# RWKV and HGRN output products: the two heads in turn, one kind of product after the other

## The chip, the cores and the metric

The kernel runs on one NeuronCore of a Trainium2 chip. The metric is the device time of one execution in microseconds (us). TensorE (PE), VectorE (DVE), ScalarE (ACT), GpSimd (POOL) and the DMA queues run side by side, each taking its own instructions in order.

## What is computed

One inference step of a two-layer streaming encoder on 512 prompt tokens and 8 sample streams of 16 tokens, with 1024 columns, all in float32. Layer 0 mixes with RWKV-7 beside forgetting attention, layer 1 with chunk attention beside HGRN2; a gated convolutional FFN follows each. The change touches the products in which RWKV and HGRN2 form their outputs from a part inside a chunk of 64 tokens and a part from the carried state:

```python
# rwkv7: one step of the scan (per head)
s = s * w_t[:, :, None, :] + sa[..., None] * b_t[:, :, None, :] + v_t[..., None] * k_t[:, :, None, :]
y_t = jnp.einsum('bhvk,bhk->bhv', s, r_t)          # sa = s @ a_t, from the state before the step
...
# hgrn2: one chunk of gla_chunkwise
o = jnp.einsum('bhts,bshv->bthv', att, vc) + jnp.einsum('bthk,bhkv->bthv', qc * jnp.exp(b), s)
```

The kernel does both scans chunk by chunk: an output chunk is (values inside the chunk times a masked score matrix) plus (carried state times scaled queries), two products added into one place in PSUM.

## The kernel before

Dense layers run through `linear` (line 359, tile `lin`), which splits each float32 operand into a high and a low float32r part and does three matmuls per block; these fill most of PE's time. Weights come through SP's queue into `wraw` (4 buffers), ACT casts them to `whi` (line 348) and DVE makes `wlo` (line 349), two buffers each.

The recurrences are cut into eight items each: four pairs of heads `p` times two halves of the tokens `hf`. A tile holds a pair of heads, head `h` in partitions `64*h` to `64*h+63`. A half has five units of 64 tokens: five prompt chunks for `hf` 0; three prompt chunks (`npu` = 3) and two units with four sample streams each for `hf` 1. A matmul here has 64 rows or columns in use, so it is given a place in the array, `tile_position=(row, column)`:

- `Y` (lines 800, 802): per chunk and head a product of all 128 rows with `SAV` at (0, 64h), form `128*64` in the profile, and one with the state `Sa` at (64h, 64h), form `64*64`. The first chunk of `hf` 0 has no state, so an `hf` 0 item has 10 + 8 products and an `hf` 1 item 6 + 6.
- `SAs` (line 817): for the sample units, a masked copy of `W1` times each of four states, four products added up, 16 in an item, all `64*64`.
- `Ys` (lines 835, 837): per unit and head one `128*64` product with `SAV` and four `64*64` ones with the states `S0`, 16 columns each: 4 + 16 in an item.
- `O` (lines 1315, 1317) and `Os` (lines 1336, 1338) are HGRN's counterparts, with `64*64` in both kinds.

A float32 product is two MATMUL instructions in the trace. An RWKV item also needs a triangular solve that leaves PE: scores `sc` on PE, a round trip through DRAM, 30 small steps on POOL (lines 681, 683), another trip, `TT` and `D` on DVE (line 755), and with these PE goes on at `P<-D,E` (line 739). The normalisation behind `Ys` goes through `mean` (line 842), behind `Os` through `ms` (line 228); the result is written to DRAM (`ydr`, `zdr`) through SP's queue and read again as `yb`, cast to `yh` by ACT (line 509) for the output projection.

A scheduler with a time model sets each engine's order when the program is built; on the chip that order is fixed.

Of the kernel before, what the change touches and what calls it, by code (L numbers as in the profile page):

```python
# [139 lines left out]
H = (slice(0, 64), slice(64, 128))  # L140
# [374 lines left out]
def mixer0(tc, A, k):  # L515
    nc = tc.nc
    V, S, G, T, dma, mm, fm, P, C = k.V, k.S, k.G, k.T, k.dma, k.mm, k.fm, k.P, k.C
# [9 lines left out]
    with tc.tile_pool(name="mx", bufs=1) as mp:  # L527
# [46 lines left out]
        def us(u):  # L574
            return slice(64 * u, 64 * u + 64)
# [11 lines left out]
        def rwkv(p, hf, r, kz, v, lrt, grt, item):  # L587
# [5 lines left out]
            def wt(name, w=HF, dt=F32):  # L593
                return mp.tile([128, w], dt, tag="w" + stage[0], name=name, bufs={"A": 11, "B": 8, "C": 5}[stage[0]])
# [5 lines left out]
            npu = 5 if hf == 0 else 3  # L600
# [3 lines left out]
            def m1(lhsT, rhs, name):  # L604
                ps = mm(name, stage[0])
                T.matmul(ps[:, 0:HF], lhsT, rhs, start=True, stop=True)
                return ps[:, 0:HF]
# [8 lines left out]
            ps = m1(blk1, rn, "kkn")  # L616
# [23 lines left out]
            AR, BK = AB[:, 0], AB[:, 1]  # L640
# [8 lines left out]
            M = ABM[:, 2:4].rearrange("p a u s t -> p (a u s t)").rearrange("p (u h s t) -> p u h s t", u=5, h=2, s=2)  # L649
            E = mp.tile([128, 5, 2, 64], F32, tag="E", name="E")  # L650
            Cc = mp.tile([128, 5, 16], F32, tag="Cc", name="Cc", bufs=2)
            for (u0, n, prompt) in (((0, 4, 1), (4, 1, 1)) if hf == 0 else ((0, 3, 1), (3, 2, 0))):
                for h in range(2):
                    ps = mm("sc", stage[0])
                    pv = ps.rearrange("p (u s t) -> p u s t", u=4, s=2)
                    for u in range(u0, u0 + n):
                        T.matmul(pv[H[h], u - u0], Bt[H[h], us(u)], AR[H[h], u], start=True, stop=True, tile_position=(64 * h, 64 * h))
                        T.matmul(pv[H[1 - h], u - u0], Kt[H[h], us(u)], AR[H[h], u], start=True, stop=True,
                                 tile_position=(64 * h, 64 * (1 - h)))
# [51 lines left out]
            SAV = mp.tile([128, 5, 2, 64], F32, tag="SAV", name="SAV", bufs=2)  # L711
            ps = mm("trA", stage[0])
# [4 lines left out]
            ps = mm("trV", stage[0])  # L717
            for u in range(5):
                for h in range(2):
                    T.matmul(ps[H[1 - h], us(u)], v[H[h], us(u)], ident[H[h], H[h]], start=True, stop=True,  # L720
                             tile_position=(64 * h, 64 * (1 - h)))
# [3 lines left out]
            for (u0, n) in ((0, 4), (4, 1)):  # L725
                ps = mm("trB", stage[0])
                pv = ps.rearrange("p (u h t) -> p u h t", u=4, h=2)
                for u in range(u0, u0 + n):
                    for h in range(2):
                        T.matmul(pv[H[h], u - u0, h, :], Bh[:, us(u)], ident[:, H[h]], start=True, stop=True, tile_position=(0, 64 * h))  # L730
                        T.matmul(pv[H[1 - h], u - u0, h, :], Kh[:, us(u)], ident[:, H[h]], start=True, stop=True,
                                 tile_position=(0, 64 * (1 - h)))
# [12 lines left out]
            ps = mm("U", stage[0])  # L745
            for u in range(5):
                for h in range(2):
                    T.matmul(ps[H[h], us(u)], M[H[1 - h], u, h, 0, :], SAV[H[1 - h], u, h, :], start=True, stop=True,
                             tile_position=(64 * (1 - h), 64 * h))
# [25 lines left out]
            Sa = [None] * 5  # L775
# [5 lines left out]
            for c in range(npu):  # L781
# [6 lines left out]
                ps = mm("Sn", stage[0])  # L788
# [8 lines left out]
            ps = mm("Y", stage[0])  # L797
            for c in range(npu):
                for h in range(2):
                    T.matmul(ps[H[h], us(c)], SAV[:, c, h, :], M[:, c, h, 1, :], start=True, stop=Sa[c] is None, tile_position=(0, 64 * h))  # L800
                    if Sa[c] is not None:
                        T.matmul(ps[H[h], us(c)], Sa[c][H[h]], AR[H[h], c, 1, :], start=False, stop=True, tile_position=(64 * h, 64 * h))  # L802
            S.copy(y[:, :npt], ps[:, :npt])
            if hf:

                S0 = mp.tile([128, NB, 64], F32, tag="S0", name="S0")
                with tc.issue_after(k.wada):
                    dma(S0, A["st_rw"][p])
                ps = mm("SAs", stage[0])
                for u in (3, 4):  # L810
                    b0 = 4 * (u - 3)
                    W1m = wt("W1m", 256)
                    V.tensor_tensor(W1m.rearrange("p (b t) -> p b t", b=4), W1[:, us(u)].unsqueeze(1).to_broadcast([128, 4, 64]),
                                    C["colb"].rearrange("p (b t) -> p b t", b=4), op=ALU.mult)
                    for h in range(2):
                        for b in range(4):
                            T.matmul(ps[H[h], us(u - 3)], W1m[H[h], 64 * b:64 * b + 64], S0[H[h], b0 + b, :], start=b == 0, stop=b == 3,
                                     tile_position=(64 * h, 64 * h))
                for h in range(2):
                    V.tensor_tensor(SAV[H[h], 3:5, h, :], ps[H[h], 0:128].rearrange("p (u t) -> p u t", u=2),  # L820
                                    W2[H[h], 192:320].rearrange("p (u t) -> p u t", u=2), op=ALU.add)
                ps = mm("Ss", stage[0])
                for u in (3, 4):
                    for h in range(2):
                        Sm = wt("Sm", 256)
                        V.tensor_tensor(Sm.rearrange("p (b v) -> p b v", b=4), SAV[:, u, h].unsqueeze(1).to_broadcast([128, 4, 64]),
                                        C["em16"].unsqueeze(2).to_broadcast([128, 4, 64]), op=ALU.mult)
                        T.matmul(ps[H[h], 256 * (u - 3):256 * (u - 2)], BK[:, u, h, :], Sm, start=True, stop=True, tile_position=(0, 64 * h))
                o = rwo[:, 1:9, :]
                G.tensor_tensor(o, S0, eL[:, 5:13].unsqueeze(2).to_broadcast([128, NB, 64]), op=ALU.mult)  # L830
                V.tensor_tensor(o, o, ps.rearrange("p (b v) -> p b v", b=NB), op=ALU.add)
                ps = mm("Ys", stage[0])
                for u in (3, 4):
                    for h in range(2):
                        T.matmul(ps[H[h], us(u - 3)], SAV[:, u, h, :], M[:, u, h, 1, :], start=True, stop=False, tile_position=(0, 64 * h))
                        for b in range(4):
                            T.matmul(ps[H[h], 64 * (u - 3) + 16 * b:64 * (u - 3) + 16 * b + 16], S0[H[h], 4 * (u - 3) + b, :],
                                     AR[H[h], u, 1, 16 * b:16 * b + 16], start=False, stop=b == 3, tile_position=(64 * h, 64 * h))
                S.copy(y[:, 192:320], ps[:, 0:128])
                dma(A["o_rw"][:, p], rwo)  # L840

# [326 lines left out]
def mixer1(tc, A, k):  # L1168
    nc = tc.nc
    V, S, G, T, dma, mm, fm, P, C = k.V, k.S, k.G, k.T, k.dma, k.mm, k.fm, k.P, k.C  # L1170
# [7 lines left out]
    def us(u):  # L1178
        return slice(64 * u, 64 * u + 64)

    k.lane.next()
    with tc.tile_pool(name="hx", bufs=1) as mp:
# [36 lines left out]
        def hgrn(p, hf, zq, zf, v, zg):  # L1219
            npu = 5 if hf == 0 else 3  # L1220
            stage = ["A"]

            def wt(name, w=HF, dt=F32):
                return mp.tile([128, w], dt, tag="w" + stage[0], name=name, bufs={"A": 16, "B": 9, "C": 7}[stage[0]])
# [19 lines left out]
            b = wt("b")  # L1244
# [33 lines left out]
            for li, m in enumerate((64, 32, 16, 8, 4, 2, 1)):  # L1278
# [15 lines left out]
                ps = each(0, n, sl(lk), sl(lq), "lev")  # L1294
# [6 lines left out]
            ps = each(0, npu, sl(kt), sl(vt), "KV", "B")  # L1301
            Sa = [None] * 5
# [9 lines left out]
            ps = mm("O", stage[0])  # L1312
            for c in range(npu):
                for h in range(2):
                    T.matmul(ps[H[h], us(c)], vt[H[h], us(c)], att[H[h], us(c)], start=True, stop=Sa[c] is None, tile_position=(64 * h, 64 * h))
                    if Sa[c] is not None:
                        T.matmul(ps[H[h], us(c)], Sa[c][H[h]], qt[H[h], us(c)], start=False, stop=True, tile_position=(64 * h, 64 * h))
            S.copy(y[:, :npt], ps[:, :npt])
            if hf:

                S0 = mp.tile([128, NB, 64], F32, tag="S0", name="S0", bufs=1)
                dma(S0, A["st_hg"][p])
                ps = mm("KVs", "B")
                for u in (3, 4):
                    vm = wt("vm", 256)
                    V.tensor_tensor(vm.rearrange("p (b v) -> p b v", b=4), vt[:, us(u)].unsqueeze(1).to_broadcast([128, 4, 64]),
                                    C["em16"].unsqueeze(2).to_broadcast([128, 4, 64]), op=ALU.mult)
                    for h in range(2):
                        T.matmul(ps[H[h], 256 * (u - 3):256 * (u - 2)], kt[H[h], us(u)], vm[H[h]], start=True, stop=True, tile_position=(64 * h, 64 * h))
                o = hgo[:, 1:9, :]  # L1330
                G.tensor_tensor(o, S0, eL[:, 5:13].unsqueeze(2).to_broadcast([128, NB, 64]), op=ALU.mult)
                V.tensor_tensor(o, o, ps.rearrange("p (b v) -> p b v", b=NB), op=ALU.add)
                ps = mm("Os", stage[0])
                for u in (3, 4):
                    for h in range(2):
                        T.matmul(ps[H[h], us(u - 3)], vt[H[h], us(u)], att[H[h], us(u)], start=True, stop=False, tile_position=(64 * h, 64 * h))
                        for j in range(4):
                            T.matmul(ps[H[h], 64 * (u - 3) + 16 * j:64 * (u - 3) + 16 * j + 16], S0[H[h], 4 * (u - 3) + j, :],
                                     qt[H[h], 64 * u + 16 * j:64 * u + 16 * j + 16], start=False, stop=j == 3, tile_position=(64 * h, 64 * h))
                S.copy(y[:, 192:320], ps[:, 0:128])  # L1340
                dma(A["o_hg"][:, p], hgo)
# [195 lines left out]
```

## Time and profile before

| | us |
|---|---|
| median of 3 runs | 2078.92 (2075.33 to 2080.8) |
| the profiled execution | 2068.11 |
| its span, first to last instruction | 2066.3 |
| PE busy | 1973.0 |
| DVE busy | 1213.5 |
| ACT busy | 944.1 |
| RWKV items (first `sc` to last `Ys`) | 98 to 594 |
| HGRN items | 1160 to 1535 |

Busy time of PE counts from an instruction's start to its modelled end, and successive matmuls overlap in it; what a group of matmuls costs is read as the distance from its first start to the next group's first start. Times of the profiled execution lie 10.8 us under the median of the runs.

### The profile page before, as it was taken

The numbers are of one execution on the slowest core, as the hardware profiler recorded it, in microseconds if no ns is written. First come the engines' busy times: TensorE is split into PE (matmuls) and PEld (weight loads), VectorE is DVE, ScalarE is ACT, GpSimd is POOL, SyncE is SP. The second block draws the span as 40 slices with busy tenths as digits, with TensorE's granted clock in tenths as the row PEclk, the third lists the DMA queues.
The fourth block names the chain that finished last, engine by engine and source line by source line (L and its number), as shares of the span: only waits on it lengthen the run. The fifth ranks groups of instructions, "written<-read, shape, count | busy, mean of one in ns | idle before, by whom it ended". The sixth has DMA issues, their size and how long they took to land.

```text
span 2066.3 us, 42482 instructions
## 1 busy us (share of the span) xinstructions
PE 1973.0 (95%) x16860; PEld 1775.5 (86%) x16860; DVE 1213.5 (59%) x2461; ACT 944.1 (46%) x1877; POOL 511.5 (25%) x1090
## 2 busy tenths in 40 slices
PE   6999999999899999999999999998999999999997
PEld 2877777766698799999999888877888999999997
DVE  3755565667667554454457625776768754454455
ACT  3633343444427442342445525555637652352444
POOL 0424352533212111121112200443223321121112
PEclk7999999989999999999999999999999999999998
DMA  8464435458534642222226786456634322222223
GB/s 311 136 221 130 156 98 151 120 122 227 154 108 161 208 141 73 72 77 77 72 83 211 240 257 195 122 147 176 215 96 133 123 72 76 78 67 77 82 80 123
DMA packets 144661, 282.51 MB, mean 137 GB/s; under 512 B 39768, under 2 KB 80064, under 8 KB 144464
## 3 DMA queue, kind: packets, MB, share of 16 engines
q1 hardware_dynamic: 136784, 267.22, 40.7%
q0 software_dynamic: 7680, 12.59, 2.8%
q8 instruction: 133, 2.18, 0.4%
q14 instruction: 64, 0.52, 0.1%
HBM read 247.69 MB, written 32.07 MB: 135 GB/s over the span
## 4 chain that ended last, share of the span: by engine, by line
PE 71%; issue 8%; DMA 8%; DVE 6%; POOL 3%; ACT 3%; SPq 0%; POOLq 0%; DVEq 0%; ACTq 0%
PE lin L359 57%; DMA wada<-in_ada_w_dram 2%; PE ada L251 1%; DVE wlo L349 1%; PE lev L1265 1%; DMA wraw<-in_w_cd_dram 1%; ACT whi L348 1%; PE Y L800 1%; POOL Tt L683 1%; PE Y L802 1%; PE av L1055 1%; DVE nt L317 1%; POOL Ttmp L681 1%; PE ptr L1048 1%; PE qk L1038 1%
## 5 line engine op out<-in xcount | busy, mean ns | idle before, releaser
L359 PE MATMUL lin<-hi,whi 128*128 128x320 f32 x2272 | 718.3, 316 | 12.6 <-ACT whi L348 7.4
L359 PE MATMUL lin<-hi,wlo 128*128 128x320 f32 x2272 | 714.1, 314 | 5.4 <-DVE wlo L349 5.3
L359 PE MATMUL lin<-lo,whi 128*128 128x320 f32 x2272 | 711.8, 314 | 0.0
L349 DVE TENSOR_TENSOR wlo<-wraw,whi 128x1024 fp32r<-128x1024 f32 (+1 forms) x272 | 335.9, 1236 | 345.3 <-ACT whi L348 342.9
L348 ACT CAST whi<-wraw 128x1024 fp32r<-128x1024 f32 (+1 forms) x272 | 279.3, 1027 | 495.0 <-PE lin L359 370.3
L359 PEld LDWEIGHTS lin<-hi,whi 128*128 128x128 f32 x2272 | 432.0, 190 | 37.6 <-ACT whi L348 10.4
L359 PEld LDWEIGHTS lin<-hi,wlo 128*128 128x128 f32 x2272 | 431.4, 190 | 20.2 <-DVE wlo L349 8.7
L359 PEld LDWEIGHTS lin<-lo,whi 128*128 128x128 f32 x2272 | 431.9, 190 | 6.4 <-issue 3.8
L359 PE MATMUL lin<-gh,whi 128*128 128x320 f32 x704 | 218.8, 311 | 2.9 <-ACT whi L348 1.7
L359 PE MATMUL lin<-gl,whi 128*128 128x320 f32 x704 | 218.1, 310 | 0.6 <-DVE gl L451 0.6
L359 PE MATMUL lin<-gh,wlo 128*128 128x320 f32 x704 | 217.9, 310 | 0.6 <-DVE wlo L349 0.5
L433 POOL COPY cvo<-u 128x2 f32<-128x2 f32 x88 | 83.3, 947 | 380.2 <-ACT u L431 380.2
L394 DVE SCALAR_TENSOR_TENSOR x<-lin,ada_cm,x 128x192 f32<-128x192 f32 (+1 forms) x160 | 76.8, 482 | 149.7 <-PE lin L359 148.9
L359 PEld LDWEIGHTS lin<-gh,whi 128*128 128x128 f32 x704 | 132.6, 189 | 4.6 <-ACT whi L348 2.8
L359 PEld LDWEIGHTS lin<-gl,whi 128*128 128x128 f32 x704 | 132.7, 189 | 1.3 <-DVE gl L451 1.1
L359 PEld LDWEIGHTS lin<-gh,wlo 128*128 128x128 f32 x704 | 132.6, 188 | 1.3 <-DVE wlo L349 1.1
L399 POOL TENSOR_TENSOR x<-x,rs 128x128 f32<-128x128 f32 x80 | 49.1, 615 | 306.9 <-DVE rs L397 306.9
L437 DVE SCALAR_TENSOR_TENSOR t<-u,pp,t 128x656 f32<-128x656 f32 x88 | 79.3, 901 | 25.8 <-ACT t L436 25.1
L251 PE MATMUL ada<-wada,csT 128*32 128x256 f32 x768 | 72.3, 422 | 19.2 <-DMA wada<-in_ada_w_dram 19.1
L359 PE MATMUL lin<-yh,whi 128*128 128x320 f32 x256 | 82.6, 325 | 3.9 <-DVE rs L397 1.4
L436 ACT ACTIVATE t<-u,pp 128x656 f32<-128x656 f32 x88 | 82.5, 938 | 7.2 <-ACT u L432 0.4
L1288 POOL TENSOR_TENSOR d<-d,q 128x160 f32<-128x160 f32 (+1 forms) x48 | 36.5, 760 | 190.6 <-ACT d L1287 186.0
(388 smaller groups left out, 3159.2 us busy)
## 6 DMA issues: line engine op xcount, KB each, us to landing
wraw<-in_w_up_dram SPq DMA_DIRECT2D x100, 512.0 KB
wada<-in_ada_w_dram SPq DMA_DIRECT2D x96, 512.0 KB
wraw<-in_w_cd_dram SPq DMA_DIRECT2D x44, 512.0 KB
wraw<-in_w_dn_dram SPq DMA_DIRECT2D x48, 448.0 KB
wraw<-in_w_ab_dram SPq DMA_DIRECT2D x40, 512.0 KB
wraw<-in_w_dn_dram SPq DMA_DIRECT2D x16, 512.0 KB
wraw<-in_w_abo_dram SPq DMA_DIRECT2D x12, 512.0 KB
wraw<-in_w_cdo_dram SPq DMA_DIRECT2D x12, 512.0 KB
```

The costliest lines, as they stand in the source:

```text
L251: T.matmul(ps[32 * j:32 * j + 32, 0:256], csT[:, kk, :], w[:, j * 256:(j + 1) * 256], start=kk == 0, stop=kk == KD - 1, tile_position=(0, ...
L317: V.tensor_tensor(t, xk(h, kk), r, op=ALU.mult)
L348: S.copy(wh[:, :w], r[:, :w])
L349: V.tensor_tensor(wl[:, :w], r[:, :w], wh[:, :w].bitcast(F32), op=ALU.subtract)
L359: T.matmul(ps[:, 0:HF], w[:, (j * nk + kk) * 128:(j * nk + kk + 1) * 128], a(h, kk), start=c == 0, stop=c == 3 * nk - 1)
L394: V.scalar_tensor_tensor(xx[:, :npr], ps[:, :npr], m[:, 16 + o, 0:1], xx[:, :npr], op0=ALU.mult, op1=ALU.add)
L399: G.tensor_tensor(xx[:, npr:], xx[:, npr:], t.rearrange("p b t -> p (b t)"), op=ALU.add)
L433: G.tensor_copy(cvo[:, o, 0, :], u[:, NP:NP + 2])
L436: S.activation(t, u[:, 2:], AF.Identity, scale=pp[:, ow + 88 + o:ow + 89 + o], bias=pp[:, ob + o:ob + o + 1])
L437: V.scalar_tensor_tensor(t, u[:, 1:UW - 1], pp[:, ow + 44 + o:ow + 45 + o], t, op0=ALU.mult, op1=ALU.add)
L681: G.tensor_tensor(tv, Tt[:, 0:n, j:j + 1].to_broadcast([40, n, w]), At[:, j:j + 1, j + 1:16].to_broadcast([40, n, w]), op=ALU.mult)
L1288: G.tensor_tensor(dv[:, :, h2:], dv[:, :, h2:], xq[:, :, h2:], op=ALU.mult)
```

## The change

Inside `Y`, first all `SAV` products of all chunks, both heads in turn, then all products with the state. The first of a head's `SAV` products alone carries `start` (it opens the whole PSUM bank of that head's partitions), the last state product `stop`. `SAs` loops over streams outside and heads inside. `Ys` does its four `SAV` products first, then the 16 with `S0`, heads innermost. `O` does both heads' first product of a chunk, then both heads' second; `Os` a unit's two first products, then its eight others with heads innermost. No product is added or taken away.

```diff
--- before.py
+++ after.py
@@ -797,9 +797,11 @@
             ps = mm("Y", stage[0])
             for c in range(npu):
                 for h in range(2):
-                    T.matmul(ps[H[h], us(c)], SAV[:, c, h, :], M[:, c, h, 1, :], start=True, stop=Sa[c] is None, tile_position=(0, 64 * h))
+                    T.matmul(ps[H[h], us(c)], SAV[:, c, h, :], M[:, c, h, 1, :], start=c == 0, stop=False, tile_position=(0, 64 * h))
+            for c in range(npu):
+                for h in range(2):
                     if Sa[c] is not None:
-                        T.matmul(ps[H[h], us(c)], Sa[c][H[h]], AR[H[h], c, 1, :], start=False, stop=True, tile_position=(64 * h, 64 * h))
+                        T.matmul(ps[H[h], us(c)], Sa[c][H[h]], AR[H[h], c, 1, :], start=False, stop=c == npu - 1, tile_position=(64 * h, 64 * h))
             S.copy(y[:, :npt], ps[:, :npt])
             if hf:
 
@@ -812,8 +814,8 @@
                     W1m = wt("W1m", 256)
                     V.tensor_tensor(W1m.rearrange("p (b t) -> p b t", b=4), W1[:, us(u)].unsqueeze(1).to_broadcast([128, 4, 64]),
                                     C["colb"].rearrange("p (b t) -> p b t", b=4), op=ALU.mult)
-                    for h in range(2):
-                        for b in range(4):
+                    for b in range(4):
+                        for h in range(2):
                             T.matmul(ps[H[h], us(u - 3)], W1m[H[h], 64 * b:64 * b + 64], S0[H[h], b0 + b, :], start=b == 0, stop=b == 3,
                                      tile_position=(64 * h, 64 * h))
                 for h in range(2):
@@ -832,10 +834,12 @@
                 ps = mm("Ys", stage[0])
                 for u in (3, 4):
                     for h in range(2):
-                        T.matmul(ps[H[h], us(u - 3)], SAV[:, u, h, :], M[:, u, h, 1, :], start=True, stop=False, tile_position=(0, 64 * h))
-                        for b in range(4):
+                        T.matmul(ps[H[h], us(u - 3)], SAV[:, u, h, :], M[:, u, h, 1, :], start=u == 3, stop=False, tile_position=(0, 64 * h))
+                for u in (3, 4):
+                    for b in range(4):
+                        for h in range(2):
                             T.matmul(ps[H[h], 64 * (u - 3) + 16 * b:64 * (u - 3) + 16 * b + 16], S0[H[h], 4 * (u - 3) + b, :],
-                                     AR[H[h], u, 1, 16 * b:16 * b + 16], start=False, stop=b == 3, tile_position=(64 * h, 64 * h))
+                                     AR[H[h], u, 1, 16 * b:16 * b + 16], start=False, stop=u == 4 and b == 3, tile_position=(64 * h, 64 * h))
                 S.copy(y[:, 192:320], ps[:, 0:128])
                 dma(A["o_rw"][:, p], rwo)
 
@@ -1313,6 +1317,7 @@
             for c in range(npu):
                 for h in range(2):
                     T.matmul(ps[H[h], us(c)], vt[H[h], us(c)], att[H[h], us(c)], start=True, stop=Sa[c] is None, tile_position=(64 * h, 64 * h))
+                for h in range(2):
                     if Sa[c] is not None:
                         T.matmul(ps[H[h], us(c)], Sa[c][H[h]], qt[H[h], us(c)], start=False, stop=True, tile_position=(64 * h, 64 * h))
             S.copy(y[:, :npt], ps[:, :npt])
@@ -1334,7 +1339,8 @@
                 for u in (3, 4):
                     for h in range(2):
                         T.matmul(ps[H[h], us(u - 3)], vt[H[h], us(u)], att[H[h], us(u)], start=True, stop=False, tile_position=(64 * h, 64 * h))
-                        for j in range(4):
+                    for j in range(4):
+                        for h in range(2):
                             T.matmul(ps[H[h], 64 * (u - 3) + 16 * j:64 * (u - 3) + 16 * j + 16], S0[H[h], 4 * (u - 3) + j, :],
                                      qt[H[h], 64 * u + 16 * j:64 * u + 16 * j + 16], start=False, stop=j == 3, tile_position=(64 * h, 64 * h))
                 S.copy(y[:, 192:320], ps[:, 0:128])
```

The order in which the built program holds PE's instructions, at the first `Y`. Before:

```order
L359 MATMUL lin<-hi_313,wlo 128x320
L800 MATMUL Y<-ABM,SAV 64x64 x3
L802 MATMUL Y<-ABM,St 64x64
L800 MATMUL Y<-ABM,SAV 64x64
L802 MATMUL Y<-ABM,St 64x64
```

Now:

```order
L359 MATMUL lin<-hi_313,wlo 128x320
L800 MATMUL Y<-ABM,SAV 64x64 x10
L804 MATMUL Y<-ABM,St 64x64 x8
L739 MATMUL TT<-T32T,P_1447 64x64 x10
L359 MATMUL lin<-hi_313,whi 128x320
```

The ten `128*64` products stand together (the row's `64x64` is the shape of its moving operand), then the eight with the state; before, the two kinds take turns from the third product on. The next item's `TT` follows both.

PE at the first `Ys` (the number in `S` is the state tile of this item). Before:

```order
L1038 MATMUL qk<-ra 128x256
L1106 MATMUL vts<-c_ident,r_6596 128x128
L835 MATMUL Ys<-ABM,SAV 64x64
L837 MATMUL Ys<-ABM,S_3883 64x16 x4
L835 MATMUL Ys<-ABM,SAV 64x64
L837 MATMUL Ys<-ABM,S_3883 64x16 x4
```

Now:

```order
L1042 MATMUL qk<-ra 128x256
L1110 MATMUL vts<-c_ident,r_6596 128x128
L837 MATMUL Ys<-ABM,SAV 64x64 x4
L841 MATMUL Ys<-ABM,S_3883 64x16 x16
L739 MATMUL W_4363<-U,TT 64x64 x10
```

Four groups of one and four, of which the first two are shown, have become one of four and one of sixteen.

The scheduler's order has also moved elsewhere. In the RWKV stretch no `lin` matmul changes its place against the items, apart from one that changes places with a `mean`, but steps of the sample attention do. In HGRN's second half the attention steps stand up to 48 `lin` matmuls earlier and the last items later: the last `Os` has 6,300 of the program's 9,696 `lin` matmuls ahead of it, where it had 6,250. ACT behind it, where the last `yh` is cast for the second output projection. Before:

```order
L348 CAST whi<-wraw 128x1024
L1216 ACTIVATE sg<-sg 128x320
L348 CAST whi<-wraw 128x1024
L509 CAST yh<-yb 128x320
L348 CAST whi<-wraw 128x1024
L295 ACTIVATE sq<-x_17870 128x320 x3
```

Now:

```order
L348 CAST whi<-wraw 128x1024
L1220 ACTIVATE sg<-sg 128x320
L348 CAST whi<-wraw 128x1024
L295 ACTIVATE sq<-x_17870 128x320 x3
L348 CAST whi<-wraw 128x1024
L295 ACTIVATE sq<-x_17870 128x320
L509 CAST yh<-yb 128x320
L348 CAST whi<-wraw 128x1024
```

The cast of `yh` has one `whi` more ahead of it, and so the first `whi` behind it belongs to a later step of the projection, 24 `lin` matmuls later. On SP some loads of `kc`, `vc` and weights have changed places with the writes of `zdr` there.

## Rows read from the trace of the kernel before

**Rows 1.** The page, part 1: engine, busy us, share of the span, instructions.

```profile
PE 1973.0 (95%) x16860; PEld 1775.5 (86%) x16860; DVE 1213.5 (59%) x2461; ACT 944.1 (46%) x1877; POOL 511.5 (25%) x1090
```

**Rows 2.** Timeline of PE, first `Y`: start, us, line, what, count of instructions.

```profile
200.79 0.45 PE L800 MATMUL Y<-ABM,SAV 128*64 128x64 f32 x6
201.16 0.32 PE L802 MATMUL Y<-ABM,St 64*64 64x64 f32 x2
201.42 0.33 PE L800 MATMUL Y<-ABM,SAV 128*64 128x64 f32 x2
...
204.86 0.22 PE L802 MATMUL Y<-ABM,St 64*64 64x64 f32 x1
204.87 0.80 PE L739 MATMUL TT<-T32T,P 64*64 64x64 f32 x19
205.59 0.41 PE L359 MATMUL lin<-hi,whi 128*128 128x320 f32 x1
```

**Rows 3.** The same view: `Y`, `SAs` and `Ys` of one second-half item.

```profile
464.29 0.33 PE L800 MATMUL Y<-ABM,SAV 128*64 128x64 f32 x2
...
467.37 0.55 PE L1048 MATMUL ptr<-c_ident,ra 128*128 128x128 f32 x3
...
469.30 1.54 PE L817 MATMUL SAs<-S,W1m 64*64 64x64 f32 x32
470.77 0.32 PE L1055 MATMUL av<-ra 128*64 128x128 f32 x1
...
479.51 0.28 PE L835 MATMUL Ys<-ABM,SAV 128*64 128x64 f32 x2
479.72 0.64 PE L837 MATMUL Ys<-ABM,S 64*64 64x16 f32 x8
...
482.75 0.66 PE L1078 MATMUL vt<-c_ident,ra 128*128 128x128 f32 x4
```

**Rows 4.** The same view: begin and end of an `O` and of an `Os`.

```profile
1179.68 0.50 PE L1315 MATMUL O<-att,vt 64*64 64x64 f32 x8
...
1180.92 0.41 PE L359 MATMUL lin<-hi,wlo 128*128 128x320 f32 x1
...
1533.56 0.41 PE L1338 MATMUL Os<-qt,S 64*64 64x16 f32 x5
...
1535.21 0.41 PE L359 MATMUL lin<-yl,whi 128*128 128x320 f32 x1
```

**Rows 5.** The same view: first and last rows of 26 `trB` instructions.

```profile
164.86 0.27 PE L731 MATMUL trB<-c_ident,Kh 128*64 128x64 f32 x1
...
165.55 0.30 PE L730 MATMUL trB<-c_ident,Bh 128*64 128x64 f32 x3
```

**Rows 6.** Stretches, PE alone: from:to us, PE busy (x), granted clock, DMA, GB/s.

```profile
318.00:321.40 3.40, 3.40 (x31) 0.50 0.00 0
...
372.70:376.10 3.40, 3.40 (x16) 0.51 0.00 0
...
434.20:437.40 3.20, 3.20 (x32) 0.50 0.32 102
...
594.60:597.90 3.30, 3.30 (x14) 0.50 0.33 99
```

**Rows 7.** Timeline of PE, POOL and DVE around two `P`: [idle before <- releaser].

```profile
494.65 0.56 PE L739 MATMUL P<-D,E 64*64 64x64 f32 x12 [0.37 <-DVE D L755]
...
484.24 0.69 POOL L706 TENSOR_TENSOR Bh<-Bt,eL 128x192 f32<-128x192 f32 x1 [7.43 <-DVE Bt L646]
...
543.51 0.49 DVE L842 SCALAR_TENSOR_TENSOR y<-mean,y 128x320 f32<-128x320 f32 x1 [3.00 <-PE mean L606]
```

**Rows 8.** Timeline of ACT and PE at the end of the second mixer.

```profile
1551.35 0.46 ACT L509 CAST yh<-yb 128x320 fp32r<-128x320 f32 x1 [2.03 <-DMA yb<-zdr]
...
1552.94 0.38 PE L359 MATMUL lin<-yh,whi 128*128 128x320 f32 x1 [1.05 <-ACT whi L348]
```

**Rows 9.** Waits of SP's queue, 1340 to 1560: us in total, times, longest.

```profile
SPq L1352 <- DVE y L1351: 22.4, 5, 9.2
```

## The prediction

> **What bounds the kernel now.** I read the page's totals first: PE is busy for 95% of the span and no other engine for more than 59% [rows 1]. Time taken from PE therefore counts, unless something stands just behind it. I then read the timeline of PE at the products concerned, not their busy time, since matmuls overlap in it. At the first `Y` the two kinds take turns, and each product's first instruction begins 0.26 us after the last product's (201.16, 201.42) [rows 2]. The next item's `TT`, right behind it on the same engine, is ten products of one form on the two diagonal places in turn: 19 of its instructions end 0.80 after the first begins. With 0.22 for one alone that is 18 steps in 0.58, so 0.032 an instruction and 0.064 a product of two; the last of them begins at 205.45 and the next form at 205.59, so 0.14 lies between runs of different forms [rows 2]. A product in `Y` costs four times a product in `TT`, with the same 64 columns. What differs is that every second one changes the form between `128*64` and `64*64`. Then I looked at the granted clock behind these bursts, and last at what stands close behind PE: the waits at `P`, at the last `yh`, and on SP.
>
> **The change, part by part.** The cost of a run of n products in one form, heads in turn, is taken as 0.064 n, and 0.14 for each change of form.
>
> `Y`, first half: 200.79 to 204.87 is 4.08 us [rows 2]; now 18 x 0.064 + 0.14 = 1.29. That is 2.8 less, 11.2 in four items. `Y`, second half: 464.29 to 467.37 is 3.08 [rows 3]; now 12 x 0.064 + 2 x 0.14 = 1.05, 2.0 less, 8.0 in four.
>
> `Ys`: 479.51 to 482.75 is 3.24 [rows 3]; now 20 x 0.064 + 0.28 = 1.56, 1.7 less, 6.7 in four. Here the 16-column products of one head now stand on one place, eight instructions in 0.64, so about 0.06 each [rows 3]. If taking turns brings nothing at 16 columns, 16 products x 2 x 0.03 x 4 items = 3.8 of the 6.7 is not had. I take the full sum, since `TT` is nearer in all but the columns, and keep the 3.8 for the range.
>
> `SAs`: 469.30 to 470.77 is 1.47 for 16 products, four on one head's place before the other's turn [rows 3]; now 16 x 0.064 + 0.14 = 1.16, so 0.3, 1.2 in four. `Os`: 1533.56 to 1535.21 is 1.65 for 19 of its 20 products [rows 4]; now 1.36, again 1.2 in four. `O`: 1179.68 to 1180.92 is 1.24 for 18 products [rows 4], and the formula gives 1.29: it already runs at that pace with two on one place, and I put it at nothing. Together 11.2 + 8.0 + 6.7 + 1.2 + 1.2 = 28.3 us of PE's time.
>
> The clock: in four stretches that begin at the end of a `Y` or a `Ys`, or within 1.2 us of it, the granted clock is 0.5, the lower level of 1.2 GHz, for about 3.4 us each [rows 6]. Before each PE had spent 3 to 4 us on products that change form. Work done at half the level loses at most half the stretch, 1.7 us, so 6.8 in all. With shorter bursts such falls should become fewer, but other small matmuls stand nearby. Between 0 and 6.8 I take half, 3.4.
>
> What is late next, in the RWKV stretch: POOL's solve and its trips through DRAM run beside PE, and `P` waits for `D`. In the first half no `Y` stands between an item's `sc` and its `P`, so a shorter `Y` moves both alike, and `lin` matmuls follow; I let all 11.2 pass. In the second half two items' `Y`, `SAs` and `Ys` (4.0 each) do stand between another's `sc` and `P`. For the first, `P` already waits 0.37 for `D` [rows 7]; its solve had stopped on POOL, which waited 7.43 for `Bt` of DVE [rows 7], and DVE in its turn takes `SAs` and `Ss` from PE. Part of the chain moves with PE; I take half as lost, 2. For the second, DVE reached `D` only after 3.00 us of waiting for `mean` of PE [rows 7], which comes earlier now; a quarter lost, 1. The bounds are 0 and 8 for the two.
>
> The end of the second mixer: the last `Os` now has 50 more `lin` matmuls ahead of it, and the first `whi` behind the last `yh` on ACT serves a step 24 matmuls later. ACT waited 2.03 for `yb`, and PE 1.05 for the `whi` behind it [rows 8]. From the end of that `Os` at 1535.21 [rows 4] to PE's restart at 1552.94 [rows 8] stand 109 `lin` matmuls, 0.15 us each without the wait. The chain now begins 7.5 later and is needed 3.6 later, so PE waits some 4 more. It could be nothing, if the sample attention ahead of it ends sooner. I take 4. The other moved attention steps and loads, in both mixers, I put at 0 with 5 to either side.
>
> Sum: 28.3 + 3.4 - 3 - 4 = 24.7, call it **25 us**. The profiled execution of 2068.1 becomes 2043; against the median of the runs, 2078.9, the time is **2054 us**. The 10.8 us between the two I carry over unchanged.
>
> **The rivals.** *The two column halves don't run side by side.* The `SAV` products of both heads use all 128 rows, so one head's weights would wait for the other's matmul, and taking turns would bring nothing. The nearest row against it is `trB`, also `128*64` on the two column halves: 26 instructions from 164.86 to 165.85, less 0.22 for the last alone, are 0.031 each [rows 5], the pace of the diagonal places. If it held all the same, the 64 products of `Y` and 16 of `Ys` would stay at 0.26, 80 x 0.196 = 15.7 of the gain would go, and the time would be 2070. The Trainium skill, "TensorE: Matmul & The Clock Gate", section "The mechanism" of its Part 3, says this: a weight load overlaps matmuls in flight only when its row group differs. The rows 5 speak against it here, for row groups of these halves are the same.
>
> *The cover is gone in RWKV's second half.* All of `Y`, `SAs`, `Ys` there, 15.9, turn into waits for DVE and POOL in attention and at `P`. For it: DVE is at 59% over the span [rows 1], and the 0.37 at `P` shows a wait with no slack left [rows 7]. Against it: the 3.00 that DVE waits for PE [rows 7]. Then 11.2 + 1.2 + 3.4 - 4 = 12 is left, and the time is 2067.
>
> *Nothing to be measured.* Each saving turns into a wait for the same chain of DRAM trips, and the end of the second mixer costs its 4: 2073 to 2085. The order shows that the change does what it says on PE, so only waits could undo it, and in the first half `lin` matmuls stand there instead.
>
> *Slower.* On SP in HGRN's second half some weight loads now stand behind writes of `zdr`, which wait for DVE, up to 9.2 us each [rows 9]. If four of them came late by that much and `lin` stood still each time, 37 us would go, 12 more than is won: 2091. It decides once a load is later than the work that the two `whi` buffers hold lasts: 2 x 24 `lin` matmuls, 7 us at 0.15, and attention's matmuls between them. So most of one wait of 9.2 is covered, and that four fall short by all of it is unlikely.
>
> **How the numbers follow.** A measurement of this kernel can tell about 0.3%, 6 us, from no change. My forecast, 2043 to 2063: 0.72. Second half without cover, 2067: 0.12. No overlap of column halves, 2070: 0.04. Nothing to be measured: 0.07. Slower: 0.05. So faster 0.88, same 0.07, slower 0.05. The lower end of the range is all 28.3 + 6.8 with the attention's 5 and no loss, 40: 2039, taken as 2040. The upper end takes in the two cases around 2070: 2070. That leaves out some 1.5 in 10.
>
> **What would show it.** In the changed profile `Y` should go from its first start to the next group's in 1.2 to 1.4 us (first half) and about 1.05 (second), `Ys` in 1.4 to 2.5, `SAs` near 1.16, `O` unchanged. If `Y` keeps over 3 us, the change of form is not what costs, and the sum falls. If they shrink and the time doesn't, PE must show new idle time at `P`, at attention's `ptr` and `av`, or at `lin` behind `whi`. The stretches at 0.5 behind `Y` and `Ys` should be fewer. The wait at the last `yh` should grow to about 5.

## The result and the profile after

The changed kernel takes 2047.38 us (median of 4 runs, 2042.21 to 2056.34); the kernel before, beside it, 2077.12 (4 runs, 2070.67 to 2080.8). The ratio is 0.9864, with a 95% interval of 0.9827 to 0.9902: 1.4% faster, by 20 to 36 us. Forecast were 2054 and a range of 2040 to 2070. The execution that was profiled took 2056.34, the longest of the four, so a difference of two single profiles shows less than the medians do.

Part 1 of the page after, beside [rows 1]:

```profile
span 2054.6 us, 42485 instructions
PE 1938.6 (94%) x16860; PEld 1748.1 (85%) x16860; DVE 1214.3 (59%) x2461; ACT 944.5 (46%) x1877; POOL 522.0 (25%) x1090
```

As many instructions on PE as before, and 34.4 us less busy time. The span is 11.7 shorter in this execution: span less busy time has grown from 93 to 116. So some of it came back as waiting (to 108 in a second profile of the changed kernel), and where it did in RWKV's stretch is shown below.

The timeline of PE after (start, us, line, what, count of instructions), at the first `Y`, which answers to [rows 2]:

```profile
205.38 0.80 PE L800 MATMUL Y<-ABM,SAV 128*64 128x64 f32 x20
206.11 0.68 PE L804 MATMUL Y<-ABM,St 64*64 64x64 f32 x16
206.63 0.46 PE L739 MATMUL TT<-T32T,P 64*64 64x64 f32 x10
```

and at `Y`, `SAs` and `Ys` of second-half items, which answer to [rows 3]:

```profile
456.87 0.57 PE L800 MATMUL Y<-ABM,SAV 128*64 128x64 f32 x12
457.36 0.56 PE L804 MATMUL Y<-ABM,St 64*64 64x64 f32 x12
457.86 0.44 PE L1052 MATMUL ptr<-c_ident,ra 128*128 128x128 f32 x2
...
470.56 0.45 PE L837 MATMUL Ys<-ABM,SAV 128*64 128x64 f32 x8 [0.41 <-DVE rwo L833]
470.94 1.11 PE L841 MATMUL Ys<-ABM,S 64*64 64x16 f32 x32
471.98 0.32 PE L1059 MATMUL av<-ra 128*64 128x128 f32 x1
...
570.89 1.15 PE L819 MATMUL SAs<-S,W1m 64*64 64x64 f32 x32
571.97 0.42 PE L359 MATMUL lin<-yh,wlo 128*128 128x320 f32 x1
```

From the first start to that of the next group `Y` now takes 1.25 us where it took 4.08 (first half), 0.99 where it took 3.08 (second half), `Ys` 1.42 where it took 3.24, `SAs` 1.08 where it took 1.47 (0.98 where another 64*64 group follows; 0.42 less is taken for all). All four first-half `Y` lie at 1.247. An `O` that runs into `lin` takes 1.195 (1.24 before). HGRN's `Os` went from 0.043 us an instruction (1.645 for 38) to 0.033 (0.865 for the last 26), about 0.4 for its 40. The sum of what the bursts lost: 4 x 2.83 + 4 x 2.09 + 4 x 1.82 + 4 x 0.42 + 4 x 0.4 = 11.3 + 8.4 + 7.3 + 1.7 + 1.6 = 30.3 us. Forecast were 28.3.

### The profile page after: what moved, and what is told of

It is laid out like the page before. It is cut to its first block, busy times and chain, and to the rows that moved or that the text cites. A ratio compares the mean times of both kernels' runs of the same rounds, so it can differ in the third digit from the quotient of the medians.

```text
span 2054.6 us, 42485 instructions
## 1 busy us (share of the span) xinstructions
PE 1938.6 (94%) x16860; PEld 1748.1 (85%) x16860; DVE 1214.3 (59%) x2461; ACT 944.5 (46%) x1877; POOL 522.0 (25%) x1090
## 5 line engine op out<-in xcount | busy, mean ns | idle before, releaser
L1292 POOL TENSOR_TENSOR d<-d,q 128x160 f32<-128x160 f32 (+1 forms) x48 | 41.8, 870 | 179.4 <-ACT d L1291 179.4
```

The lines of the kernel that those rows point to most:

```text
L1292: G.tensor_tensor(dv[:, :, h2:], dv[:, :, h2:], xq[:, :, h2:], op=ALU.mult)
```

## Experiments

Nine kernels ran besides. Each was timed beside the kernel before on the same chip. In the table the gain is what the ratio lacks of 1, times the median of before there, with its 95% interval; "bursts" is what the starts in that kernel's own trace say the products lost, in all. The last column is an estimate. Each execution has its granted clock on record, so (1 - granted clock) x span is what the clock withheld. Over 123 executions, each compared with others of its kernel and chip, a microsecond withheld goes with 0.82 us of time. That part is taken off each time, and the means of the two kernels are compared, with two standard errors to either side.

| kernel | bursts, us | ratio | gain, us | gain without the clock's part, us |
|---|---|---|---|---|
| the whole change | 30.3 | 0.9846 (0.9809 to 0.9883) | 32.0 (24 to 40) | 23.3 (20 to 27) |
| RWKV's part | 28.7 | 0.9865 (0.9825 to 0.9905) | 28.0 (20 to 36) | 19.5 (16 to 23) |
| HGRN's part | 1.6 | 1.0007 (0.9974 to 1.0041) | -1.5 (-9 to 5) | 2.2 (-1 to 5) |
| `Y` alone | 19.7 | 0.9901 (0.9862 to 0.9940) | 20.5 (12 to 29) | 15.9 (12 to 19) |
| `Y` by chunk, `SAs`, `Ys` | 22.8 | 0.9863 (0.9828 to 0.9898) | 28.5 (21 to 36) | 14.9 (11 to 18) |
| kinds together, heads apart | 20.2 | 0.9899 (0.9869 to 0.9929) | 21.0 (15 to 27) | 12.0 (9 to 15) |
| `Y` of the first half | 11.3 | 0.9922 (0.9893 to 0.9950) | 16.2 (10 to 22) | 11.9 (9 to 15) |
| `Y` of the second half, `SAs`, `Ys` | 17.4 | 0.9921 (0.9887 to 0.9956) | 16.4 (9 to 23) | 9.3 (6 to 13) |
| kinds alternating, heads crossed | 9.0 | 0.9931 (0.9901 to 0.9961) | 14.3 (8 to 21) | 6.2 (3 to 9) |

The theory: PE pays for each change of form, TensorE is what the end waits for, so what the bursts lose the time loses. In all nine rows the bursts lie within the interval of the gain. But two further terms hide in that agreement and nearly cancel, as the last column shows: part of what the bursts lose comes back as waiting, most of it in the second half, and about as much is won because the clock is withheld less. Both are told under "What passes to the end".

### The change and its parts

The whole change on another chip:

> The changed kernel as it is, beside its parts on the same chip. By the theory (a change of form of the array costs about 0.2 us, the parts' times add up, and what TensorE saves reaches the end) the bursts give, by the trace of the changed kernel, 4 x (4.08 - 1.25) + 4 x (3.08 - 0.99) + 4 x (3.24 - 1.42) + 4 x (1.47 - 1.05) + about 1 in HGRN = 30 us: 2047 to 2049 where the kernel before takes 2077.

Measured were 2044.43 against 2075.13. The theory's 2047 to 2049 lies within the interval, which is 7 to 8 us wide to either side.

RWKV's three places as in the change, HGRN's `O` and `Os` as before. The edit, against the changed kernel, undoes these two:

```
                     T.matmul(ps[H[h], us(c)], vt[H[h], us(c)], att[H[h], us(c)], ...
-                for h in range(2):
                     if Sa[c] is not None:
...
-                    for j in range(4):
-                        for h in range(2):
+                        for j in range(4):
                             T.matmul(ps[H[h], 64 * (u - 3) + 16 * j:...
```

> The change in RWKV alone (Y, SAs, Ys); HGRN's O and Os as before. Theory of the form change: 28 to 29 us less than the kernel before, the whole change but for 1 to 2 us. Rival, that the order of the second mixer is worth as much as the bursts (the instructions that the scheduler moves there): the kernel gives back 5 us or more of the whole change, or beats it by as much.

HGRN's two places as in the change, RWKV's as before:

> The change in HGRN alone (O in pairs of heads, Os with the heads in turn); RWKV as before. No change of form is removed here. Theory of the form change: Os is some 0.3 us shorter four times, O 0.04 us: 0 to 2 us less, same within what can be measured. Rival, that taking turns of heads is what pays: by the number of products set in turn (32 of Os and 28 of O against 28 of Y, 32 of Ys and 32 of SAs) it would bring about two thirds of the gain of RWKV's part, some 15 us. Rival, that the moved whi and yh casts at the end of the second mixer cost: 3 to 5 us more than before.

RWKV's part has the gain: 28.0 us. HGRN's has none that can be told: -1.5, with 15 us far outside the interval, so turns of heads by themselves pay little. A small cost of the moved instructions there is not excluded by an interval of -9 to 5; the whole change and RWKV's part differ by 4 us with 8 to either side, which doesn't settle it.

`Y` alone, the first hunk of the change:

```
             for c in range(npu):
                 for h in range(2):
-                    T.matmul(ps[H[h], us(c)], SAV[:, c, h, :], ..., start=True, stop=Sa[c] is None, ...)
+                    T.matmul(ps[H[h], us(c)], SAV[:, c, h, :], ..., start=c == 0, stop=False, ...)
+            for c in range(npu):
+                for h in range(2):
                     if Sa[c] is not None:
```

> RWKV's Y alone, the products of one kind together; all else as before. Theory of the form change: 4 x 2.83 + 4 x 2.09 = 19.7 us less than before, if what is saved in the second half passes as well. Rival, that the second half's savings are swallowed by the chain behind (the wait of P for D): 11 us less. Rival, that the gain comes from fewer stretches at half clock: no fixed share of the whole gain, and the stretches behind Y stay away here as in the whole change.

Two thirds of RWKV's bursts, and 20.5 of its 28.0 us. The rival by which only the first half's 11 pass falls outside the interval of 12 to 29, if barely.

### How the cost goes with the number of changes

`Y` grouped only within a chunk: both heads' `SAV` products, then both heads' state products. `SAs` and `Ys` as in the change, HGRN as before.

```
             for c in range(npu):
                 for h in range(2):
                     T.matmul(ps[H[h], us(c)], SAV[:, c, h, :], M[:, c, h, 1, :], start=True, stop=Sa[c] is None, ...)
+                for h in range(2):
                     if Sa[c] is not None:
                         T.matmul(ps[H[h], us(c)], Sa[c][H[h]], AR[H[h], c, 1, :], start=False, stop=True, ...)
```

> The whole of RWKV's and none of HGRN's part, but with Y's kinds grouped only within a chunk: both heads' SAV products, then both heads' state products, chunk after chunk. Y keeps 7 changes of form in the first half (15 before, 1 with the change) and 5 in the second (11 before, 1 with the change). Theory (0.2 us for each change of form, in proportion): bursts of 1.25 + 6 x 0.2 = 2.45 us and 0.99 + 4 x 0.2 = 1.8 us; 4 x 1.2 + 4 x 0.8 = 8 us slower than the change, 22 us faster than before. Rival, that what costs is returning to the same output region of PSUM right after a product into it (before, each state product follows the SAV product into its own chunk and head at once): here one product lies between, so most of the cost is gone, bursts below 1.6 and 1.25 us.

The bursts came out at 2.13 us and 1.58: neither the theory's 2.45 and 1.8 nor the rival's 1.6 and 1.25. The timeline of PE at a second-half `Y` of this kernel shows why:

```profile
454.70 0.34 PE L800 MATMUL Y<-ABM,SAV 128*64 128x64 f32 x4
454.97 0.33 PE L803 MATMUL Y<-ABM,St 64*64 64x64 f32 x4
455.23 0.34 PE L800 MATMUL Y<-ABM,SAV 128*64 128x64 f32 x4
...
456.02 0.33 PE L803 MATMUL Y<-ABM,St 64*64 64x64 f32 x4
456.28 0.44 PE L1051 MATMUL ptr<-c_ident,ra 128*128 128x128 f32 x2
```

A run of two products in one form (four instructions) takes 0.26 us, as does a run of a single one in the kernel before (two instructions: 201.16 to 201.42 in [rows 2]). Within the runs the starts lie 7, 101 and 6 ns apart and 150 at the change for two products of two heads, and 107 and 150 for a lone one: behind a change the second instruction of a place comes 0.1 us after the first, and the other head's product fits into that gap. So the price is not a fixed 0.2 for each change. It is 0.147 for each change while a run has both heads (this kernel against the change: six changes more for 0.88 us, four more for 0.59), and the first grouping, from one product to two, brings more, 0.25 for each change removed. The forecast's unit of 0.14 was right for runs of two and more; my expectation here had averaged the two kinds of saving.

### Form or place

Kinds together, heads apart: all products of head 0, then all of head 1, of each kind. `SAs` and HGRN as before.

```
+            for h in range(2):
+                for c in range(npu):
+                    T.matmul(ps[H[h], us(c)], SAV[:, c, h, :], M[:, c, h, 1, :], start=c == 0, stop=False, ...)
+            for h in range(2):
+                for c in range(npu):
+                    if Sa[c] is not None:
+                        T.matmul(ps[H[h], us(c)], Sa[c][H[h]], AR[H[h], c, 1, :], start=False, stop=c == npu - 1, ...)
...
                 ps = mm("Ys", stage[0])
-                for u in (3, 4):
-                    for h in range(2):
+                for h in range(2):
+                    for u in (3, 4):
                         T.matmul(ps[H[h], us(u - 3)], SAV[:, u, h, :], M[:, u, h, 1, :], start=u == 3, ...)
-                        for b in range(4):
+                for h in range(2):
+                    for u in (3, 4):
+                        for b in range(4):
```

> Y and Ys with the kinds together (one change of form each, as in the change), but the heads apart: all products of head 0, then all of head 1, of each kind. SAs, O and Os as before. Theory, that the form is what costs and turns of heads bring little: by SAs (0.42 us for 32 products in turn against apart, 0.013 each) Y 1.25 + 18 x 0.013 = 1.5 us, Y second half 1.15, Ys 1.42 + 20 x 0.013 = 1.7 us; 25 to 26 us faster than before. Rival, that the turns of heads pay (a place of the array that is loaded anew while its last product streams waits for it): the bursts stay above 2 us (first half) and Ys above 2.3, and a third or more of the gain is lost, 15 to 18 us faster than before.

The timeline of PE at a second-half `Y` of this kernel, beside 456.87 to 457.86 of the changed one:

```profile
459.98 0.73 PE L800 MATMUL Y<-ABM,SAV 128*64 128x64 f32 x12
460.64 0.73 PE L804 MATMUL Y<-ABM,St 64*64 64x64 f32 x12
461.30 0.32 PE L1059 MATMUL av<-ra 128*64 128x128 f32 x1
```

1.32 us, where heads in turn take 0.99 and the kernel before 3.08. The first half takes about 1.9 (1.25 and 4.08), `Ys` 2.15 (1.42 and 3.24). So in `Y` the form is most of it, 1.76 of 2.09 and 2.2 of 2.83, and turns of heads the rest; in `Ys`, with 16 products of 16 columns, turns are 0.73 of 1.82. The bounds of the two theories stood at 1.7 and 2.3 for `Ys`: it lies between. Taking turns brings about 0.03 us a product at 64 columns and 0.036 in `Ys`. The time, 21.0 with an interval of 15 to 27, holds the theory's 25 to 26 and the rival's 15 to 18 alike and doesn't decide.

Kinds alternating at every product as before, but a state product never behind a `SAV` product of its own head. `SAs` and `Ys` as in the change, HGRN as before.

```
+            seq = [(0, c, h) for c in range(npu) for h in range(2) if Sa[c] is None]
+            full = [c for c in range(npu) if Sa[c] is not None]
+            for a in range(2):
+                seq += [(s, c, a ^ s) for c in full for s in range(2)]
+            for i, (s, c, h) in enumerate(seq):
...
```

> As the whole of RWKV's part and none of HGRN's, but with Y's kinds alternating at every product as before (15 changes of form in the first half, 11 in the second), and with the heads crossed: SAV product of head 0, state product of head 1, and so on through the chunks, then the other way round. So no state product follows a SAV product into the same place of the array or the same part of PSUM, and the heads take turns at each product. Theory (only the form counts: the trace of the kernel before has 152 and 149 ns at a change into a product of the same head and into one of the other head): no gain in Y, bursts 4.1 us and 3.1 us as before; only SAs and Ys gain, 4 x (0.42 + 1.82) = 9 us faster than before. Rival (following a product into its own place or its own part of PSUM is what costs the larger share): 1.12 + 15 x 0.147 = 3.3 us and 0.74 + 11 x 0.147 = 2.4 us, 14 to 15 us faster than before. Rival (turns of heads are what pays): bursts near the change's 1.25 and 0.99, the change's full gain.

The timeline of PE at a second-half `Y` of this kernel:

```profile
465.91 0.33 PE L807 MATMUL Y<-ABM,SAV 128*64 128x64 f32 x2
466.17 0.32 PE L805 MATMUL Y<-ABM,St 64*64 64x64 f32 x2
466.43 0.33 PE L807 MATMUL Y<-ABM,SAV 128*64 128x64 f32 x2
...
468.74 0.33 PE L805 MATMUL Y<-ABM,St 64*64 64x64 f32 x2
468.99 0.33 PE L1055 MATMUL ptr<-c_ident,ra 128*128 128x128 f32 x1
```

3.08 us from 465.91 to 468.99, to the hundredth what [rows 3] have; the shortest of the first-half bursts takes 4.09, where 4.08 stood. Here the heads take turns at every product but one, no product follows another into its own place and part of PSUM, and it brings nothing. Nor is it the flags that the change also moves: this kernel sets `start` and `stop` once for each head, as the changed one does. What costs is the form. The gain in time, 14.3 with an interval of 8 to 21, holds both the theory's 9 and the rival's 14 to 15, so the verdict rests on the bursts alone.

### What passes to the end

The first half's `Y` grouped, the second half's as before, under `if hf:`, and the reverse with `SAs` and `Ys`:

```
+            if hf:
+                for c in range(npu):
...
+            else:
+                for c in range(npu):
...
```

> Y in the first half alone, the four groups where TensorE waited for nothing behind them. Theory: 4 x 2.83 = 11.3 us faster than before, all of it passes. Rival, that the clock takes part of it: below 8.

> The rest of RWKV's part: Y in the second half, SAs and Ys; Y of the first half as before. The bursts shrink by 4 x (2.09 + 0.42 + 1.82) = 17.3 us. Theory (nearly all passes, but for two waits of P for D): 14 to 17 us faster than before, and with the first half's kernel the two gains add up to that of RWKV's part. Rival, that the chain through D, POOL and the loads of the next item swallows it: TensorE's idle time before P, trB and sc grows by half of what is saved, 5 to 9 us faster than before.

First 16.2, second 16.4; together 32.6, where RWKV's part has 28.0 and its bursts 28.7. By the time alone the second half's gain is inside the theory's 14 to 17 and, at its lower end, touches the rival's 9. But its waits did grow. PE's waits from 400 to 620 us, in the changed kernel:

```profile
engine line waited for: us in total, times, longest us
PE P L739 <- DVE D L755: 6.5, 3, 3.3
PE vts L1110 <- DMA r<-fv: 3.4, 2, 2.8
PE W L739 <- ACT W L767: 2.4, 1, 2.4
```

and in the kernel before:

```profile
PE sav L1146 <- ACT r L1141: 3.1, 2, 2.6
PE P L739 <- DVE D L755: 3.0, 2, 2.7
```

`P` waits 3.5 us more for `D`, `vts` and `W` wait anew, `sav` no more: about 6 us by these rows. That is not all of it. PE's busy time from the first `Y` to the first of the second half, and from there to the end of the last `Ys`, before and after:

```profile
core 0: us, PE busy (x), PEclk, DMA share, GB/s
200.79:414.13 213.34, 206.52 (x2134) 0.97 0.43 130
414.13:593.54 179.41, 170.19 (x1904) 0.95 0.57 155
...
205.38:409.57 204.19, 194.21 (x2134) 0.98 0.46 136
409.57:581.98 172.41, 154.73 (x1903) 0.94 0.61 161
```

The length of a stretch less PE's busy time in it is what PE stood still: 9.2 us in the second half, and now 17.7 (16.9 in the other profile of the changed kernel), 6.8 in the first, and now 10.0 (8.7). The eleven profiles agree: 8.2 to 9.2 in the second half where its `Y` is as before, 13.9 to 17.9 where it is grouped; in the first 6.2 to 7.2 and 7.7 to 10.6. So about half of the second half's 17.4 comes back as waiting, and 2 to 3 of the first half's 11.3. The last column of the table agrees: 9.3 of 17.4 for the second half, 11.9 against 11.3 for the first. The mechanism is the rival's, which had 5 to 9 us; the theory's 14 to 17 was reached by time only with what the clock gave back.

By that column the clock is why the first half's gain in time is larger than its 11.3. The granted clock (PEclk) in stretches at the end of the first-half `Y`, first in the kernel that changes only the second half:

```profile
core 0: us, PE busy (x) PEld busy (x) DVE busy (x) ACT busy (x) POOL busy (x), PEclk, DMA share, GB/s
203.80:207.20 3.40, 3.40 (x32) 3.05 (x31) 1.38 (x3) 0.61 (x2) 0.00 (x0) 0.50 0.00 0
261.80:265.20 3.40, 3.40 (x31) 3.17 (x31) 2.12 (x6) 0.89 (x2) 0.32 (x2) 0.50 0.00 1
323.30:326.70 3.40, 3.40 (x31) 3.19 (x30) 2.43 (x4) 0.42 (x1) 0.00 (x0) 0.51 0.00 0
```

and then in the one that changes only the first half, behind three of its `Y`:

```profile
203.00:206.40 3.40, 3.40 (x46) 3.25 (x40) 1.48 (x4) 1.69 (x3) 0.02 (x1) 1.00 0.12 48
311.30:314.70 3.40, 3.40 (x44) 3.33 (x41) 2.41 (x4) 1.81 (x3) 0.00 (x0) 1.00 0.01 4
365.70:369.10 3.40, 3.40 (x38) 3.33 (x33) 3.19 (x9) 1.36 (x4) 2.09 (x3) 1.00 0.53 167
```

In the four kernels whose first-half `Y` alternates (before, HGRN's part, second half, crossed) the clock fell to 0.5, the lower level of 1.2 GHz, within 1.4 us of the end of 13 of the 16 bursts, after some 4 us of products that change form; in the seven whose first-half `Y` is grouped (the changed one's two profiles among them), behind none of 28. Ten of the falls last 3.4 us and three 6.8, and PE is busy in those shown, so one of 3.4 costs up to 1.7. From 100 to 400 us the first four have 21.4 us at the lower level in the mean, the seven 10.2: half the difference is 5.6 us. Over the whole span it is 112.8 against 103.0, 4.9. A single profile doesn't show it (the profiled pair has 115.3 and 105.2, with 16 falls and 18), because other falls come and go, most of them behind waits of PE.

The second half has such falls too. In the eleven profiles, behind the first 100 us, 25 falls begin without a wait of PE ahead of them (at most 0.12 us idle in the 7 us before). Thirteen are those named; the other 12 lie within 1.3 us of the end of a second-half `Y` or `Ys` that still alternates, and the five profiles in which both are grouped have none. The executions' granted clocks bear it out: with the whole change the clock withheld 48.4 us of the span in the mean, with the kernel before on the same chip 57.4, so 9.0 less, with 6 to either side. The first half by itself has 5.3 less withheld, the second half by itself 10.4.

## Why the prediction was right

**What bounds.** Right for the greater part: TensorE's own time, in stretches where `lin` and attention follow at once. All nine kernels gained what their bursts lost, within their intervals; without the clock's part the whole change gained 23.3 of its 30.3 us.

**The terms of the bursts.** `Y` was put at 1.29 and 1.05 and took 1.25 and 0.99; `Ys` 1.56 against 1.42; `SAs` 1.16 against 1.08 or less; `O` unchanged within 0.05. 28.3 were to be won, 30.3 were. The unit from `TT`, 0.064 a product and 0.14 a change, holds for runs in which both heads appear; a run of a single product costs 0.26, as the forecast had read it directly. The doubt about 16 columns (3.8 of the 6.7 in `Ys`) was unfounded: `Ys` runs at the same pace, and heads apart would have cost 0.73 x 4 = 2.9 of it.

**The clock.** 3.4 were taken from between 0 and 6.8. The place was right: the falls at the end of `Y` and `Ys` are gone. The size was too small. Profiles put the term at up to 5, the granted clocks of all executions at about 7 (0.82 x 9.0), though with 5 to either side. The forecast counted four falls in one profile of the kernel before, and that execution was 10.8 us under the median; the profile of HGRN's part, near its median, has eight.

**The second half's losses.** 3 were taken from between 0 and 8. Of the two places named, the first was put at 2 and the second at 1. At the first `P` waits about as before; the second, `P` of the last item, did get the wait:

```profile
535.73 0.91 PE L739 MATMUL P<-D,E 64*64 64x64 f32 x12 [3.35 <-DVE D L755]
```

Before, the timeline shows no wait of `P` there; [rows 7] have the 3.00 that DVE still waited for PE then. The loss was thus put in the wrong one of the two. With `W` and the attention steps, whose moves the forecast had put at 0, PE's idle time in the second half grew by about 8 us, where 3 stood. In the first half, where all 11.2 were to pass, it grew by 2 to 3.

**The end of the second mixer.** This term was wrong altogether. 4 us were to be lost at the last `yh`, and PE doesn't wait there. ACT after, beside [rows 8]:

```profile
1545.01 1.05 ACT L348 CAST whi<-wraw 128x1024 fp32r<-128x1024 f32 x1 [0.29 <-PE lin L359]
1545.96 0.46 ACT L295 ACTIVATE sq<-x 128x320 f32<-128x320 f32 x1
1547.61 0.46 ACT L509 CAST yh<-yb 128x320 fp32r<-128x320 f32 x1 [1.18 <-DMA yb<-zdr]
1548.53 1.05 ACT L348 CAST whi<-wraw 128x1024 fp32r<-128x1024 f32 x1 [0.46 <-PE lin L359]
```

The cast of `whi` behind the last `yh` had PE waiting for 1.05 before; now it waits itself, 0.46, for PE to give a buffer back. The step that failed is the count "serves a step 24 matmuls later". In ACT's whole order two casts of `whi` more stand ahead of the last `yh` than before, not one: the piece that I read held only one of them. So it is needed 48 matmuls later, and against 50 `lin` matmuls more ahead of the last `Os` nothing is left. Before, 17.7 us lay between the end of that `Os` (1535.21) and PE's restart behind the wait; now 1532.19 is the end of `Os`, `yh` begins 15.4 later, and `lin` runs on:

```profile
1548.43 0.31 PE L359 MATMUL lin<-yh,whi 128*128 128x320 f32 x1
```

**The sum.** With the terms as they were measured, 30.3 + 7 - 8 - 2 = 27, where 24.7 stood. The medians moved by 29.7, with 8 to either side. That the forecast came so near is luck in part. It had the waits some 7 us too small and counted 4 for the second mixer that weren't lost; it had the clock some 4 and the bursts 2 too small. These errors nearly cancel.

**The rivals.** *Column halves that don't run side by side* fell: 12 `SAV` instructions of all 128 rows take 0.49 us to the next group in turn and 0.66 with the heads apart, so taking turns helps them as it does the state products (0.50 and 0.66). The Trainium skill ("TensorE: Matmul & The Clock Gate", Part 3, "The mechanism") has a weight load overlap matmuls in flight only when the row groups differ. The two column halves use the same ones, so by that rule taking turns would bring nothing; 0.49 against 0.66 decides against it here. *The cover gone in the second half* fell: `Y` alone gained 20.5, and the second half by itself 16.4. But about half of that rival's mechanism is there: 8 of some 17 us turned into waits. *Nothing to be measured* fell. *Slower*, by SP's queue: from 1370 to 1560 us it waits 12.2 us in 3 for `y`, where it was 14.1 in 4, and the longest is 9.2 as in [rows 9]; PE's waits for `whi` there are 2.3, where they were 4.6. It did not happen.

## What to carry to other kernels

Where small matmuls of two array forms alternate, look at the distance between their starts, not at their busy time, and write all products of a form as one run with the places in turn: in this kernel each change cost 0.15 to 0.25 us, as much as two to four products. Grouping in pairs already brought some seven tenths of it in `Y` (1.95 of 2.83, 1.50 of 2.09). What a moved cast or load does at the far end of a stretch should be counted over the engine's whole order, since a piece of it can hold half of the move. And a time that agrees with the sum can hide two terms that cancel: the idle time of the engine and the granted clock, looked at one by one, told of both here.

## What was not expected of the hardware

A lone product and a pair of products on two places cost the same 0.26 us between changes of form. Whether the next form uses the same place or another makes no difference: 3.08 us both ways. At the lower clock level the alternating product takes 1.6 times as long. In the crossed kernel the rows of a `Y` at a granted clock of 0.50 lie 0.41 and 0.40 apart, where 0.26 is the distance at 1.00:

```profile
419.20:422.60 3.40, 3.40 (x18) 2.46 (x18) 2.54 (x7) 1.54 (x6) 1.04 (x3) 0.50 0.36 64
...
419.19 0.48 PE L807 MATMUL Y<-ABM,SAV 128*64 128x64 f32 x2
419.60 0.47 PE L805 MATMUL Y<-ABM,St 64*64 64x64 f32 x2
420.00 0.47 PE L807 MATMUL Y<-ABM,SAV 128*64 128x64 f32 x2
```
